# Compression matmuls in four column groups of the array, and another order of work where two blocks meet

## The chip, the cores and the metric

One Trainium2 chip, one of its cores. The metric is the device time of one execution in microseconds (us). Between runs of this kernel the time varies by about 0.05%.

## What is computed

Two layers, each a mixer and an MLP, over 256 positions of width 2048, in float32. The mixer projects the normalised input into the heads of four kinds of attention, runs them, and projects back. The part that the change touches first is the compression of the first kind:

```python
blk = np.arange(n_c)[:, None] * NSA_CMP_STRIDE + np.arange(NSA_CMP_BLOCK)[None, :]

def compress(t, pe, w1, w2):
    tb = (t[:, blk] + pe).reshape(b, n_c, NSA_CMP_BLOCK * d)
    return jax.nn.gelu(tb @ w1) @ w2

kc = compress(k_cmp, pe_k, cmp_k1, cmp_k2)
vc = compress(v_cmp, pe_v, cmp_v1, cmp_v2)
```

There are 15 blocks of 32 positions with stride 16, d is 128, and w1 has 32 x 128 rows and 256 columns. So `tb @ w1` is a sum over 32 positions of a 15 x 128 by 128 x 256 product, done for keys and for values in both layers. The second part of the change lies where a block ends in `x = x + _rms_norm(...)` and the next begins with `hin = _rms_norm(x, g)` and a product with its first weights.

## The kernel before

All weights come from memory in granules of at most 128 x 1024 float32 (`Granule`), in the order in which they are used. `load` issues their DMAs on SP into six `raw` buffers. `prep` splits a granule into two tiles, `hi` and `lo`, in a format that TensorE multiplies in one pass: `split_hi` (L190) copies raw to hi on ACT, and `split_lo` (L193) subtracts on DVE. There are six hi and six lo buffers, and `ready(g, look)` sees to it that everything up to `look` granules ahead of g is split. The normalised input is kept in the same way in the tiles `HL`, high half and low half of each chunk. A product with weights is then hi x (high and low input together, 512 columns, L424) and lo x high input (256 columns, L429).

The program is written out in full when it is built, in a fixed order on each engine. A list `work` gives the granules' order. `run_gran` takes one granule: it first lets waiting work of the vector engines go on (`fill("v")`), then readies and multiplies, then lets waiting small matmuls go on (`fill("pe")`). Small work (evacuations, attention, norms) is written as generators (`Chain`) that these calls advance.

**Compression.** `cmp_units` gives 8 granules for each of keys and values in each layer, 32 in all, and `mixer` puts one of them after every second granule of the projections. `build_t2` adds pe to the 15 blocks' inputs and writes for each position 32 columns into a tile `T2`, 15 high parts and 15 low parts. A compression granule holds four positions. For each, two matmuls take 128 columns of T2 from the position's first on as stationary operand and hi or lo (256 columns) as moving one, and all accumulate in one bank (L1060):

```python
for w in (g.hi, g.lo):
    TE.matmul(box["a"][:, :256], lhsT=lt, rhs=w[:, j * 256:(j + 1) * 256],
```

Rows 0 to 31 of the bank are used: `cmp_tail` copies them to `hs` (L1075), adds the high parts' rows and the low parts' by a float32 matmul with the constant `sel` (L1080, 32 rows), applies gelu and multiplies by w2.

**Joins.** `start_block` begins a block. The first is `run_first`; the three others are `lead`, whose pieces run between the last matmuls of the block before. x is held in two tiles (t = 0 and 1) of four chunks of 512 columns. `res` adds the block's result to a chunk of x on DVE, `t_in` transposes it on TensorE (L376), `hl_in` makes HL of it on ACT and DVE (L384, L385), and `sq_in` squares it on ACT for the norm (L391). The block's first three units are multiplied as their parts become ready: `mm_t` and `mm_lo` (L461, L465) with chunks 0 and 1, `mm_w` (L416, L417, L419) with chunks 2 and 3. After the last of them `finish` launches `rows`: DVE sums the squares (L485, L313), POOL takes the power and makes a diagonal tile (L314, L488), TensorE spreads it over all partitions with a float32 matmul (L493), and ACT copies the result to `r2bc` (L495). The units' evacuations (L906 on ACT and L908 on DVE in a mixer) follow.

Of the kernel before, what the change touches and what calls it, by code (L numbers as in the profile page):

```python
# [56 lines left out]
def _const_tables():  # L57
# [16 lines left out]
    for b in range(15):  # L74
        sel[b, b] = 1.0
        sel[16 + b, b] = 1.0
    put("sel", sel)
# [30 lines left out]
class Granule:  # L108
    __slots__ = ("src", "n", "uses", "raw", "hi", "lo", "idx")

    def __init__(self, src, n):
        self.src, self.n, self.uses = src, n, 1

# [23 lines left out]
def hybrid_kernel(ctx, tc, a):  # L137
# [26 lines left out]

    def gran(src, c0, n):
        return Granule(src[:, c0:c0 + n], n)

# [11 lines left out]
    def load(upto):  # L179
        while state["load"] <= min(upto, len(grans) - 1):  # L180
            g = grans[state["load"]]
            g.raw = wp.tile([128, 1024], F32, tag="raw", name="raw", bufs=RAW_BUFS)
            nc.sync.dma_start(out=g.raw[:, :g.n], in_=g.src)
            state["load"] += 1
# [14 lines left out]
    def prep(upto, how=split):  # L199
        while state["gran"] <= min(upto, len(grans) - 1):  # L200
            i = state["gran"]
            if i >= HL_BUFS and grans[i - HL_BUFS].uses > 0:
                return
            g = grans[i]
            load(i + RAW_BUFS - 1)
            g.hi, g.lo = split_tiles()
            how(g, 0, g.n)
            state["gran"] += 1
# [266 lines left out]
    def start_block(site, src, evacs, mg, mg_extra=None):  # L475
# [25 lines left out]
        def finish(accs, first):  # L501
            scaled[0] = False
            launch(rows())
            for i in range(len(us)):
                launch(evacs[i](accs[i], first and first[i]))
# [36 lines left out]
        def lead():  # L542
# [41 lines left out]
            split_lo(gs[2, 0], 0, 1024)  # L584
            prep(gs[0, 1].idx, split_hi)
            t_in(2, 0)
            t_in(2, 1)
            hl_in(site, 2)
            split_lo(gs[0, 1], 0, 1024)
            for i in range(n):  # L590
# [4 lines left out]
            prep(gs[1, 1].idx)  # L595
            res(mg, 3, 1)
            accs = [bank() for _ in us]
            for c in (2, 3):
                for i in range(n):
                    g = gs[i, 1]  # L600
                    ready(g, 4)
                    mm_w(accs[i], g, 4 * c, 4 * c + 4, 8, EARLY)
                    used(g)
                    if c == 2 and i == 0:
                        t_in(3, 0)
                        t_in(3, 1)
                        hl_in(site, 3)
                    for q in {(2, 1): ((0, 1), (1, 1)), (2, 2): ((2, None), (3, 0)), (3, 0): ((3, 1),)}.get((c, i), ()):
                        sq_in(q[0], (0, 1) if q[1] is None else q[1:])
            finish(accs, first)  # L610
# [246 lines left out]
    def mixer(l):  # L857
# [5 lines left out]
        def open_pool():  # L863
# [6 lines left out]
            st["oT"] = [mp.tile([128, 256], F32, name=f"oT{k}") for k in range(KT)]  # L870
            st["T2"] = [mp.tile([128, 608], F32R, name=f"T2{i}") for i in range(2)]
            for t_ in st["T2"]:
                GP.memset(t_.bitcast(F32), 0.0)
            st["Pc"] = [scr([128, 4, 128], f"Pc{i}") for i in range(2)]
# [151 lines left out]
        def build_t2(kind, half):  # L1026
            yield "v", dict(scr=1)
            src = st["kc" if kind == 0 else "vc"]
            tmp = scr([128, 16, 16], "t2tmp")
            v_ = src[:, 16 * half:16 * half + 240].rearrange("p (b s) -> p s b", s=16)  # L1030
            pe = st["pe"][:, kind, 16 * half:16 * half + 16].unsqueeze(2).to_broadcast([128, 16, 15])
            V.tensor_tensor(tmp[:, :, :15], v_, pe, op=OP.add)
            T = st["T2"][half]
            t3 = T[:, :512].rearrange("p (s c) -> p s c", c=32)
            V.tensor_copy(t3[:, :, 0:15], tmp[:, :, :15])
            V.tensor_tensor(t3[:, :, 16:31], tmp[:, :, :15], t3[:, :, 0:15].bitcast(F32), op=OP.subtract)
            st["T2", kind, half] = True
            drop("scr")
            if half:
                drop("qk")  # L1040

        def cmp_units(kind):
            box = {}

            def make(u4):
                u = a["cmp1"][l, kind, u4]
                for h in range(2):
                    g = gran(u, h * 1024, 1024)

                    def run(g=g, p0=8 * u4 + 4 * h):  # L1050
                        def emit():
# [4 lines left out]
                            for j in range(4):  # L1056
                                pos = p0 + j
                                lt = st["T2"][pos // 16][:, (pos % 16) * 32:(pos % 16) * 32 + 128]
                                for w in (g.hi, g.lo):
                                    TE.matmul(box["a"][:, :256], lhsT=lt, rhs=w[:, j * 256:(j + 1) * 256],  # L1060
                                              start=(pos == 0 and w is g.hi), stop=(pos == 31 and w is g.lo))
                        run_gran(g, 0.85, emit)
# [9 lines left out]
        def cmp_tail(kind, p):  # L1072
            yield "v", dict(scr=1)
            hs = scr([128, 512], "hs")
            SC.activation(hs[:32, :256], p[:32, :256], AF.Copy)  # L1075
            drop("ps")
            yield "pe", dict(ps=1)
            q = bank()
            for j in range(2):
                TE.matmul(q[:, j * 128:(j + 1) * 128], lhsT=hs[:32, j * 128:(j + 1) * 128],  # L1080
                          rhs=C("sel")[:32], start=True, stop=True)
            yield "v"
# [532 lines left out]
```

## Time and profile before

| | |
|---|---|
| time, median of 3 runs | 2319.83 us (2318.98 to 2320.26) |
| the profiled execution's own time | 2319.57 us |
| span of its profile | 2317.4 us |
| PE, weight loads, DVE, ACT, POOL busy | 99%, 86%, 74%, 52%, 2% of the span |
| granted TensorE clock, mean | 0.999 |
| bytes moved | 437.57 MB, 189 GB/s |

The span runs from the first to the last instruction in the trace; the time has what lies around it as well. PE is TensorE's multiplying, PEld its loading of weights, which overlaps with it. The end of a matmul is modelled in the trace and overlaps with the next one's start, so what a matmul takes of TensorE's stream is read from the distance between starts, or from the chain of waits, which gives each piece of time to one instruction.

### The profile page before, as it was taken

The numbers are of one execution on the slowest core, as the hardware profiler recorded it, in microseconds if no ns is written. First come the engines' busy times: TensorE is split into PE (matmuls) and PEld (weight loads), VectorE is DVE, ScalarE is ACT, GpSimd is POOL, SyncE is SP. The second block draws the span as 40 slices with busy tenths as digits, with TensorE's granted clock in tenths as the row PEclk, the third lists the DMA queues.
The fourth block names the chain that finished last, engine by engine and source line by source line (L and its number), as shares of the span: only waits on it lengthen the run. The fifth ranks groups of instructions, "written<-read, shape, count | busy, mean of one in ns | idle before, by whom it ended". The sixth has DMA issues, their size and how long they took to land.

```text
span 2317.4 us, 33362 instructions
## 1 busy us (share of the span) xinstructions
PE 2298.9 (99%) x12476; PEld 1994.7 (86%) x12476; DVE 1720.3 (74%) x2936; ACT 1202.1 (52%) x1947; POOL 51.0 (2%) x71
## 2 busy tenths in 40 slices
PE   8999999999999999999999999999999999999998
PEld 8888888888888888888888888888888888888887
DVE  6967656798888888565588676568988888885655
ACT  6654555644444444555466545555444444444553
POOL 1000000100000000000010000001000000000000
PEclk9999999999999999999999999999999999999999
DMA  8764456556555555656557644564666555555563
GB/s 275 253 217 136 147 170 202 167 190 201 191 191 185 189 190 184 200 187 210 173 180 237 208 146 155 173 194 155 201 200 192 190 190 191 184 193 197 193 200 116
DMA packets 122659, 437.57 MB, mean 189 GB/s; under 512 B 13888, under 2 KB 14016, under 8 KB 122496
## 3 DMA queue, kind: packets, MB, share of 16 engines
q1 hardware_dynamic: 120384, 429.40, 56.3%
q0 software_dynamic: 1824, 5.94, 0.8%
q8 instruction: 98, 1.61, 0.3%
q14 instruction: 65, 0.53, 0.1%
q10 hardware_dynamic: 288, 0.10, 0.0%
HBM read 433.28 MB, written 2.10 MB: 188 GB/s over the span
## 4 chain that ended last, share of the span: by engine, by line
PE 96%; DVE 2%; ACT 1%; issue 1%; POOL 0%; DMA 0%; SPq 0%; DVEq 0%; POOLq 0%; ACTq 0%
PE bank L424 36%; PE bank L429 19%; PE bank L715 9%; PE bank L713 9%; PE bank L714 9%; PE bank L665 2%; PE bank L667 2%; PE bank L666 2%; PE bank L1060 1%; PE bank L1137 1%; DVE lo L193 1%; PE bank L417 1%; DVE x L405 0%; PE bank L461 0%; ACT trash L391 0%
## 5 line engine op out<-in xcount | busy, mean ns | idle before, releaser
L193 DVE TENSOR_TENSOR lo<-raw,hi 128x1024 fp32r<-128x1024 f32 (+1 forms) x818 | 984.6, 1210 | 489.2 <-ACT hi L190 484.1
L190 ACT ACTIVATE hi<-raw 128x1024 fp32r<-128x1024 f32 (+1 forms) x818 | 847.2, 1046 | 410.8 <-PE bank L715 265.4
L424 PE MATMUL bank<-HL,hi 128*128 128x512 f32 x3648 | 881.8, 392 | 0.0
L424 PEld LDWEIGHTS bank<-HL,hi 128*128 128x128 f32 x3648 | 668.5, 188 | 128.5
L429 PEld LDWEIGHTS bank<-HL,lo 128*128 128x128 f32 x3648 | 470.0, 191 | 18.1
L429 PE MATMUL bank<-HL,lo 128*128 128x256 f32 x3648 | 480.7, 283 | 0.0
L713 PE MATMUL bank<-hi,xs 128*128 128x512 f32 x960 | 374.4, 390 | 0.0
L715 PE MATMUL bank<-hi,xs 128*128 128x512 f32 x960 | 373.6, 389 | 0.0
L714 PE MATMUL bank<-lo,xs 128*128 128x512 f32 x960 | 373.5, 389 | 0.0
L715 PEld LDWEIGHTS bank<-hi,xs 128*128 128x128 f32 x960 | 180.2, 188 | 37.6
L714 PEld LDWEIGHTS bank<-lo,xs 128*128 128x128 f32 x960 | 180.2, 188 | 37.2
L713 PEld LDWEIGHTS bank<-hi,xs 128*128 128x128 f32 x960 | 180.2, 188 | 37.0
L1486 DVE SCALAR_TENSOR_TENSOR cv<-u,cw,cv 128x255 f32<-128x255 f32 x352 | 170.2, 483 | 12.5
L1472 ACT ACTIVATE u<-bank 128x256 f32<-128x256 f32 x176 | 66.6, 381 | 207.6 <-PE bank L424 196.1
L1492 ACT ACTIVATE gl<-cv 128x256 f32<-128x256 f32 x88 | 36.8, 418 | 217.8 <-DVE cv L1486 217.7
L665 PE MATMUL bank<-hi,HL 128*128 128x512 f32 (+1 forms) x256 | 97.3, 380 | 1.5 <-DVE qk L908 1.5
L667 PE MATMUL bank<-hi,HL 128*128 128x512 f32 (+1 forms) x256 | 93.6, 366 | 0.0
L666 PE MATMUL bank<-lo,HL 128*128 128x512 f32 (+1 forms) x256 | 93.3, 365 | 0.0
L1480 DVE TENSOR_TENSOR u<-u,r2bc 128x256 f32<-128x256 f32 x176 | 74.9, 426 | 5.7
L1483 DVE TENSOR_SCALAR cv<-u,cw 128x256 f32<-128x256 f32 x176 | 72.7, 413 | 6.4
L1474 DVE TENSOR_TENSOR u<-u,bank 128x256 f32<-128x256 f32 x176 | 72.9, 414 | 0.0
L686 DVE TENSOR_TENSOR xs<-y,xs 128x256 fp32r<-128x256 f32 x176 | 72.2, 418 | 0.0
(216 smaller groups left out, 1486.7 us busy)
## 6 DMA issues: line engine op xcount, KB each, us to landing
raw<-in_w_up SPq DMA_DIRECT2D x352, 512.0 KB, 4.3
raw<-in_w_down SPq DMA_DIRECT2D x176, 512.0 KB, 3.7
raw<-in_w_cols SPq DMA_DIRECT2D x122, 512.0 KB, 4.3
raw<-in_w_out SPq DMA_DIRECT2D x64, 512.0 KB, 4.1
raw<-in_w_v SPq DMA_DIRECT2D x48, 512.0 KB, 4.0
raw<-in_cmp SPq DMA_DIRECT2D x32, 512.0 KB, 5.0
gpost<-in_gpost POOLq DMA_DIRECT2D x8, 512.0 KB, 6.4
raw<-in_w_x SPq DMA_DIRECT2D x8, 408.0 KB, 4.6
```

The lines of the kernel that those rows point to most:

```text
L190: SC.activation(g.hi[:, c0:c0 + n], g.raw[:, c0:c0 + n], AF.Copy)
L193: eng.tensor_tensor(g.lo[:, c0:c0 + n], g.raw[:, c0:c0 + n], g.hi[:, c0:c0 + n].bitcast(F32), op=OP.subtract)
L424: TE.matmul(o, lhsT=g.hi[:, k % 8 * 128:k % 8 * 128 + 128], rhs=HL[k // 4][:, k % 4, :], start=(k == 0), stop=(k == KT - 1))
L429: TE.matmul(o[:, :256], lhsT=g.lo[:, k % 8 * 128:k % 8 * 128 + 128], rhs=hview(k), start=False, stop=False)
L665: TE.matmul(o, lhsT=h, rhs=wh, start=(K == 0), stop=False)
L666: TE.matmul(o, lhsT=h, rhs=wl, start=False, stop=False)
L667: TE.matmul(o, lhsT=lo, rhs=wh, start=False, stop=(K == KT - 1))
L713: TE.matmul(o, lhsT=h_, rhs=wh, start=(k[1] == 0), stop=False)
L714: TE.matmul(o, lhsT=h_, rhs=wl, start=False, stop=False)
L715: TE.matmul(o, lhsT=l_, rhs=wh, start=False, stop=(k[1] == nk - 1))
L1480: V.tensor_tensor(u, u, r2bc, op=OP.mult)
L1486: V.scalar_tensor_tensor(cv[:, n:], u[:, :256 - n], w[:, tap:tap + 1], cv[:, n:], op0=OP.mult, op1=OP.add)
```

## The change

A compression granule is no longer split. It is marked `whole`, its four positions are multiplied straight from `raw` in float32, each with a 32-column piece of T2 into 32 partitions of the bank of its own, so each of the four uses 32 columns of the array. T2 holds float32 values, 16 columns a position. `cmp_tail` copies all 128 rows and `sel` adds four partial sums. A load into the raw buffer of a whole granule is written only after that granule's matmuls. In `lead`, squares and one `split_lo` stand earlier, `ready` looks two granules ahead instead of four at one place, and `rows` is launched and advanced once after the second-last `mm_w` instead of in `finish`.

```diff
     for b in range(15):
-        sel[b, b] = 1.0
-        sel[16 + b, b] = 1.0
+        sel[b::32, b] = 1.0
...
     def load(upto):
         while state["load"] <= min(upto, len(grans) - 1):
-            g = grans[state["load"]]
+            i = state["load"]
+            if i >= RAW_BUFS and grans[i - RAW_BUFS].whole and grans[i - RAW_BUFS].uses > 0:
+                return
+            g = grans[i]
...
             load(i + RAW_BUFS - 1)
-            g.hi, g.lo = split_tiles()
-            how(g, 0, g.n)
+            if state["load"] <= i:
+                return
+            if not g.whole:
+                g.hi, g.lo = split_tiles()
+                how(g, 0, g.n)
...
         def finish(accs, first):
-            scaled[0] = False
-            launch(rows())
+            if first is None:
+                scaled[0] = False
+                launch(rows())
...
             prep(gs[0, 1].idx, split_hi)
+            sq_in(0, (1,))
+            split_lo(gs[0, 1], 0, 1024)
             t_in(2, 0)
             t_in(2, 1)
             hl_in(site, 2)
-            split_lo(gs[0, 1], 0, 1024)
...
             res(mg, 3, 1)
+            sq_in(1, (1,))
             accs = [bank() for _ in us]
+            after = {(2, 0): ((2, 0),), (2, 1): ((3, 0), (2, 1)), (2, 2): ((3, 1),)}
             for c in (2, 3):
                 for i in range(n):
                     g = gs[i, 1]
-                    ready(g, 4)
+                    ready(g, 4 if i or c == 3 else 2)
                     mm_w(accs[i], g, 4 * c, 4 * c + 4, 8, EARLY)
                     used(g)
...
-                    for q in {(2, 1): ((0, 1), (1, 1)), (2, 2): ((2, None), (3, 0)), (3, 0): ((3, 1),)}.get((c, i), ()):
-                        sq_in(q[0], (0, 1) if q[1] is None else q[1:])
+                    for q, t in after.get((c, i), ()):
+                        sq_in(q, (t,))
+                    if c == 3 and i == 1:
+                        scaled[0] = False
+                        launch(rows())
+                        fill("v")
             finish(accs, first)
...
-            st["T2"] = [mp.tile([128, 608], F32R, name=f"T2{i}") for i in range(2)]
+            st["T2"] = [mp.tile([128, 320], F32, name=f"T2{i}") for i in range(2)]
...
-            V.tensor_tensor(tmp[:, :, :15], v_, pe, op=OP.add)
-            T = st["T2"][half]
-            t3 = T[:, :512].rearrange("p (s c) -> p s c", c=32)
-            V.tensor_copy(t3[:, :, 0:15], tmp[:, :, :15])
-            V.tensor_tensor(t3[:, :, 16:31], tmp[:, :, :15], t3[:, :, 0:15].bitcast(F32), op=OP.subtract)
+            T = st["T2"][half][:, :256].rearrange("p (s c) -> p s c", c=16)
+            V.tensor_tensor(T[:, :, 0:15], v_, pe, op=OP.add)
...
-                                pos = p0 + j
-                                lt = st["T2"][pos // 16][:, (pos % 16) * 32:(pos % 16) * 32 + 128]
-                                for w in (g.hi, g.lo):
-                                    TE.matmul(box["a"][:, :256], lhsT=lt, rhs=w[:, j * 256:(j + 1) * 256],
-                                              start=(pos == 0 and w is g.hi), stop=(pos == 31 and w is g.lo))
+                                c = (p0 + j) % 16 * 16
+                                TE.matmul(box["a"][32 * j:32 * j + 32, :256], lhsT=st["T2"][p0 // 16][:, c:c + 32],
+                                          rhs=g.raw[:, j * 256:(j + 1) * 256], start=(p0 == 0), stop=(p0 == 28))
...
-            SC.activation(hs[:32, :256], p[:32, :256], AF.Copy)
+            SC.activation(hs[:, :256], p[:, :256], AF.Copy)
...
-                TE.matmul(q[:, j * 128:(j + 1) * 128], lhsT=hs[:32, j * 128:(j + 1) * 128],
-                          rhs=C("sel")[:32], start=True, stop=True)
+                TE.matmul(q[:, j * 128:(j + 1) * 128], lhsT=hs[:, j * 128:(j + 1) * 128],
+                          rhs=C("sel"), start=True, stop=True)
```

The lines of the changed kernel are shifted: its L1066 is the compression matmul, L429 and L434 are L424 and L429 of before, L195 is L193, L390 is L385, L410 is L405, L490 is L485.

On TensorE, at the first compression granule, before:

```order
L424 MATMUL bank<-HL_123,hi 128x512 x4
L1060 MATMUL bank<-hi,T_105 128x256
L1060 MATMUL bank<-lo,T_105 128x256
L1060 MATMUL bank<-hi,T_105 128x256
L1060 MATMUL bank<-lo,T_105 128x256
L1060 MATMUL bank<-hi,T_105 128x256
L1060 MATMUL bank<-lo,T_105 128x256
L1060 MATMUL bank<-hi,T_105 128x256
L1060 MATMUL bank<-lo,T_105 128x256
L424 MATMUL bank<-HL_120,hi 128x512 x4
```

and now:

```order
L434 MATMUL bank<-HL_122,lo 128x256 x4
L434 MATMUL bank<-HL_123,lo 128x256 x4
L429 MATMUL bank<-HL_122,hi 128x512 x4
L429 MATMUL bank<-HL_123,hi 128x512 x4
L1066 MATMUL bank<-raw,T_105 32x256 x4
L429 MATMUL bank<-HL_120,hi 128x512 x4
```

Eight matmuls that write all 128 rows have become four that write 32 rows each, in the same place between two runs of 512-column matmuls.

On DVE, at the join from mixer 0 to MLP 0, before (HL_4163 and HL_4164 are chunks 2 and 3 of the input):

```order
L440 SCALAR_TENSOR_TENSOR HL_4162<-bank,gpre,HL_4162 128x128 x4
L193 TENSOR_TENSOR lo<-raw,hi 128x1024
L385 SCALAR_TENSOR_TENSOR HL_4163<-bank,gpre,HL_4163 128x256 x4
L193 TENSOR_TENSOR lo<-raw,hi 128x1024 x2
L405 SCALAR_TENSOR_TENSOR x_69<-mg_4112,rr_78,x_69 128x512
L193 TENSOR_TENSOR lo<-raw,hi 128x1024 x3
L385 SCALAR_TENSOR_TENSOR HL_4164<-bank,gpre,HL_4164 128x256 x4
L193 TENSOR_TENSOR lo<-raw,hi 128x1024 x2
L485 TENSOR_REDUCE r_82<-ss_76 128x2
```

and now (chunks 2 and 3 are HL_4023 and HL_4024):

```order
L445 SCALAR_TENSOR_TENSOR HL_4022<-bank,gpre,HL_4022 128x128 x4
L195 TENSOR_TENSOR lo<-raw,hi 128x1024 x2
L390 SCALAR_TENSOR_TENSOR HL_4023<-bank,gpre,HL_4023 128x256 x4
L195 TENSOR_TENSOR lo<-raw,hi 128x1024
L410 SCALAR_TENSOR_TENSOR x_69<-mg_3972,rr_78,x_69 128x512
L195 TENSOR_TENSOR lo<-raw,hi 128x1024
L390 SCALAR_TENSOR_TENSOR HL_4024<-bank,gpre,HL_4024 128x256 x4
L195 TENSOR_TENSOR lo<-raw,hi 128x1024 x3
L490 TENSOR_REDUCE r_82<-ss_76 128x2
```

One lo has moved ahead of chunk 2, and two have moved from before chunk 3 to behind it.

On ACT, at the join from MLP 0 to mixer 1, before (L391 are the squares, L906 the copy out of an accumulator):

```order
L190 ACTIVATE hi<-raw 128x1024
L384 ACTIVATE HL_11140<-bank,gpre 128x256 x4
L190 ACTIVATE hi<-raw 128x1024 x4
L384 ACTIVATE HL_11141<-bank,gpre 128x256 x4
L190 ACTIVATE hi<-raw 128x816
L391 ACTIVATE trash,ss_76<-x_69 128x512 x2
L391 ACTIVATE trash,ss_76<-x_68 128x512
L391 ACTIVATE trash,ss_76<-x_69 128x512
L391 ACTIVATE trash,ss_76<-x_68 128x512
L391 ACTIVATE trash,ss_76<-x_69 128x512
L190 ACTIVATE hi<-raw 128x816
L1388 ACT_TABLE_LOAD
```

and now (the squares are L396, hi is L192, the HL pieces L389):

```order
L192 ACTIVATE hi<-raw 128x1024
L396 ACTIVATE trash,ss_76<-x_69 128x512
L389 ACTIVATE HL_11000<-bank,gpre 128x256 x4
L192 ACTIVATE hi<-raw 128x1024
L396 ACTIVATE trash,ss_76<-x_69 128x512
L192 ACTIVATE hi<-raw 128x1024
L389 ACTIVATE HL_11001<-bank,gpre 128x256 x4
L396 ACTIVATE trash,ss_76<-x_68 128x512
L192 ACTIVATE hi<-raw 128x1024 x2
L192 ACTIVATE hi<-raw 128x816
L396 ACTIVATE trash,ss_76<-x_68 128x512
L396 ACTIVATE trash,ss_76<-x_69 128x512 x2
```

Of the six squares that stood together, three now stand ahead of them, between other pieces of work.

## Rows read from the trace of the kernel before

**Rows 1.** The page, part 1: busy time, share of the span, instructions.
```profile
PE 2298.9 (99%) x12476; PEld 1994.7 (86%) x12476; DVE 1720.3 (74%) x2936; ACT 1202.1 (52%) x1947; POOL 51.0 (2%) x71
```

**Rows 2.** The page, part 4: the chain that ended last, by engine.
```profile
PE 96%; DVE 2%; ACT 1%; issue 1%; POOL 0%; DMA 0%; SPq 0%; DVEq 0%; POOLq 0%; ACTq 0%
```

**Rows 3.** The chain in order of time, compression of layer 0: start us, us, what.
```profile
51.97 1.84 PE bank L424 x8
53.80 0.97 PE bank L1060 x8
54.77 1.84 PE bank L424 x8
...
60.37 0.97 PE bank L1060 x8
```

**Rows 4.** PE's groups of instructions: count, busy us, mean ns, idle before.
```profile
L1060 PE MATMUL bank<-hi,T 128*128 128x256 f32 x128 | 32.3, 285 | 0.0
L1060 PE MATMUL bank<-lo,T 128*128 128x256 f32 x128 | 31.8, 282 | 0.0
```

**Rows 5.** The chain in order of time: three places with float32 matmuls.
```profile
108.61 0.45 PE bank L1137 x4
...
111.85 0.86 PE bank L1137 x4
...
195.91 0.22 PE bank L1244 x2
```

**Rows 6.** The timeline there: start us, us, engine, line, form, [idle before].
```profile
101.74 0.52 PEld L1080 LDWEIGHTS bank<-cst,hs 32*128 32x128 f32 x4 [0.35 <-issue]
...
111.69 1.02 PE L1137 MATMUL bank<-qk 128*128 128x256 f32 x4
...
195.77 0.36 PE L1244 MATMUL bank<-nlf,cst 128*128 128x4 f32 x2
```

**Rows 7.** The chain in order of time, around one L1080.
```profile
99.97 1.84 PE bank L424 x8
101.81 0.64 PE bank L1080 x4
102.45 1.58 PE bank L424 x6
```

**Rows 8.** The page, part 5: the splits (busy us, mean ns of one, idle before).
```profile
L193 DVE TENSOR_TENSOR lo<-raw,hi 128x1024 fp32r<-128x1024 f32 (+1 forms) x818 | 984.6, 1210 | 489.2 <-ACT hi L190 484.1
L190 ACT ACTIVATE hi<-raw 128x1024 fp32r<-128x1024 f32 (+1 forms) x818 | 847.2, 1046 | 410.8 <-PE bank L715 265.4
```

**Rows 9.** DMA issues of compression weights, and busy us of each engine, 53 to 113 us.
```profile
raw<-in_cmp SPq DMA_DIRECT2D x32, 512.0 KB, 5.0
...
53.00:113.00 60.00, 60.00 (x374) 53.90 (x373) 54.72 (x116) 36.40 (x60) 0.00 (x0) 1.00 0.75 255
```

**Rows 10.** The timeline at the first join, chunk 2.
```profile
432.96 2.35 DVE L193 TENSOR_TENSOR lo<-raw,hi 128x1024 fp32r<-128x1024 f32 x2
...
433.41 0.39 PE L417 MATMUL bank<-HL,hi 128*128 128x512 f32 x1
...
434.23 0.39 PE L419 MATMUL bank<-HL,lo 128*128 128x256 f32 x1 [0.43 <-DVE lo L193]
```

**Rows 11.** The timeline at the first join, chunk 3.
```profile
435.89 3.49 DVE L193 TENSOR_TENSOR lo<-raw,hi 128x1024 fp32r<-128x1024 f32 x3
...
439.32 0.28 PE L416 MATMUL bank<-HL,lo 128*128 128x256 f32 x1
439.83 0.50 PE L417 MATMUL bank<-HL,hi 128*128 128x512 f32 x1 [0.23 <-DVE HL L385]
...
440.56 0.28 PE L416 MATMUL bank<-HL,lo 128*128 128x256 f32 x1
440.86 0.50 PE L417 MATMUL bank<-HL,hi 128*128 128x512 f32 x1
```

**Rows 12.** The timeline of POOL at the first join.
```profile
448.58 0.72 POOL L314 TENSOR_TENSOR r<-r,cst 128x2 f32<-128x2 f32 x1 [19.83 <-DVE r L313]
449.40 2.69 POOL L488 TENSOR_SCALAR diag<-cst,r 128x128 f32<-128x128 f32 x2
```

**Rows 13.** The timeline at the second join: ACT, DVE and PE.
```profile
1177.36 0.62 ACT L391 ACTIVATE trash<-x 128x512 bf16<-128x512 f32 x1
...
1181.67 0.19 ACT L391 ACTIVATION_READ_ACCUMULATOR trash<-x 128x1 f32 x1
...
1185.68 1.93 DVE L193 TENSOR_TENSOR lo<-raw,hi 128x816 fp32r<-128x816 f32 x2 [1.73 <-ACT hi L190]
...
1186.26 0.29 PE L667 MATMUL bank<-hi,HL 128*128 128x272 f32 x1
...
1187.53 0.41 DVE L908 TENSOR_TENSOR qk<-qk,bank 128x256 f32<-128x256 f32 x1
...
1188.09 0.36 PE L665 MATMUL bank<-hi,HL 128*128 128x272 f32 x1 [1.54 <-DVE qk L908]
```

More of the change, by code (lines that the diff above doesn't have):

```diff
@@ L108, with __init__ @@
 class Granule:
-    __slots__ = ("src", "n", "uses", "raw", "hi", "lo", "idx")
-    def __init__(self, src, n):
-        self.src, self.n, self.uses = src, n, 1
+    __slots__ = ("src", "n", "uses", "raw", "hi", "lo", "idx", "whole")
+    def __init__(self, src, n, whole=False):
+        self.src, self.n, self.uses, self.whole = src, n, 1, whole
 class Chain:
@@ L163, in hybrid_kernel, with gran @@
     state = dict(load=0, gran=0)
-    def gran(src, c0, n):
-        return Granule(src[:, c0:c0 + n], n)
+    def gran(src, c0, n, whole=False):
+        return Granule(src[:, c0:c0 + n], n, whole)
     def add(f, *gs):
@@ L870, in open_pool @@
             st["oT"] = [mp.tile([128, 256], F32, name=f"oT{k}") for k in range(KT)]
-            st["T2"] = [mp.tile([128, 608], F32R, name=f"T2{i}") for i in range(2)]
+            st["T2"] = [mp.tile([128, 320], F32, name=f"T2{i}") for i in range(2)]
             for t_ in st["T2"]:
-                GP.memset(t_.bitcast(F32), 0.0)
+                GP.memset(t_, 0.0)
             st["Pc"] = [scr([128, 4, 128], f"Pc{i}") for i in range(2)]
@@ L1026, in build_t2 @@
         def build_t2(kind, half):
-            yield "v", dict(scr=1)
+            yield "v"
             src = st["kc" if kind == 0 else "vc"]
-            tmp = scr([128, 16, 16], "t2tmp")
             v_ = src[:, 16 * half:16 * half + 240].rearrange("p (b s) -> p s b", s=16)
             pe = st["pe"][:, kind, 16 * half:16 * half + 16].unsqueeze(2).to_broadcast([128, 16, 15])
-            V.tensor_tensor(tmp[:, :, :15], v_, pe, op=OP.add)
-            T = st["T2"][half]
-            t3 = T[:, :512].rearrange("p (s c) -> p s c", c=32)
-            V.tensor_copy(t3[:, :, 0:15], tmp[:, :, :15])
-            V.tensor_tensor(t3[:, :, 16:31], tmp[:, :, :15], t3[:, :, 0:15].bitcast(F32), op=OP.subtract)
+            T = st["T2"][half][:, :256].rearrange("p (s c) -> p s c", c=16)
+            V.tensor_tensor(T[:, :, 0:15], v_, pe, op=OP.add)
             st["T2", kind, half] = True
-            drop("scr")
             if half:
@@ L1047, in make @@
                 for h in range(2):
-                    g = gran(u, h * 1024, 1024)
+                    g = gran(u, h * 1024, 1024, True)
                     def run(g=g, p0=8 * u4 + 4 * h):
```

## The prediction

> **What bounds the kernel now.** I read the busy times first: TensorE is busy for 2298.9 of 2317.4 us [rows 1]. The chain of work that ended last says the same: 96% of it is PE, and no other engine has more than 2% [rows 2]. So what the change takes from TensorE's own stream is gained in full, what it takes from ACT or DVE is gained only where TensorE waits for them, and the places to read are two: the compression's matmuls and the joins between blocks. The profiled execution took 2319.57 us around its span of 2317.4; the median of the runs shown is 2319.83. I sum against the first and add the 0.26 us at the end. A measurement of this kernel can tell about 0.2% from no change, that is 4.6 us.
>
> In the compression, a granule (four positions) is eight matmuls and takes 0.97 us of TensorE, with unbroken work on both sides [rows 3]. There are 256 such matmuls, so 32 granules [rows 4]: 31 us in all.
>
> **The change, part A: four column groups.** A granule becomes four float32 matmuls of 256 columns into 32 array columns each. What a float32 matmul costs here is seen at L1137: two of them with 256 columns are four passes and take 0.86 us, so a pass takes 0.215 us and each matmul two passes [rows 5, 6]. Four matmuls are eight passes: 1.72 us one after another, and 0.43 us if the four groups run beside each other. Everything hangs on which, and no row of this trace shows column groups, so I bound it from both sides.
>
> What the trace does show is a change of the array's shape. The L1080 matmuls use 32 of 128 rows. Four of their passes take 0.64 us, where four ordinary passes of 128 columns take 0.45 [rows 5, 7]; and the six matmuls behind them take 1.58 us where six of eight that took 1.84 would be 1.38 [rows 7]. That is 0.19 us on the way in and 0.20 on the way out, 0.39 for the pair. On the way in the weights stand in the open (the weight loader was idle for 0.35 us before them [rows 6]). A load of 128 columns costs 0.11, as L1244 shows, whose two passes move 4 columns each and still take 0.22 [rows 5, 6]. With 32 columns I estimate a quarter, 0.03, so 0.19 becomes 0.11 and the pair 0.31. The change now pays this pair at each of the 32 granules, where before there was none. The Trainium skill, "TensorEngine Tiling (Array Packing)", section "Tiling Modes", says that a change of tiling mode drains TensorE; the 0.39 us at L1080 agrees, and without that rule the sum would be 32 times 0.31, 9.9 us, lower.
>
> With the groups beside each other the last group starts six load-and-pass steps after the first: 6 x 0.03 = 0.17 us (0.11 each would be 0.66, the far bound). A granule is then 0.31 + 0.17 + 0.43 = 0.91 us, against 0.97: 32 x -0.06 = **-1.9 us**. Its bounds are 0.43 us (no drain, no steps: -17.3 us) and 2.03 us (all eight passes in a row: +33.9 us). I take the lower half because the four groups write different partitions of one bank and share no weights.
>
> The end of each compression (four in all) now multiplies 128 instead of 32 rows of hs. The passes have the same columns, but the pair of shape changes goes: 4 x -0.39 = **-1.6 us**. The copy into hs has as many elements per partition as before.
>
> The hi and lo passes of 32 granules go: 1.05 us of ACT and 1.2 of DVE each [rows 8]. I count them at nothing, because TensorE has no gap in the compression [rows 3]. In return a whole granule keeps its raw buffer until TensorE has read it, and every later load queues behind it on SP. Six places later comes the next compression granule but one, some 13 us on (53.80 to 60.37 is one period) [rows 3]; a load lands 5.0 us after issue [rows 9], and the two ordinary ones behind it, by 3 x 512 KB at the 255 GB/s of that stretch [rows 9], some 4 us later, then hi and lo. That leaves about 2 us, so nothing is added; if the reserve were 1 us short instead, TensorE would lose up to 1 us at each of the 32 granules. build_t2 loses two DVE operations, and the T2 memsets on POOL shrink; nothing waits for either.
>
> **Part B: the joins.** There are three (after mixer 0, MLP 0 and mixer 1), all alike but for one wait. At the first, L419 starts 0.82 us after the L417 before it instead of 0.23: it waits for the lo of the first second-half granule, which DVE computes after the four L385 of chunk 2 [rows 10]. The change puts that lo first, into a stretch where DVE waits for ACT; the loss of 0.59 goes. Then the first L417 of chunk 3 starts 0.51 us after its L416 instead of 0.12, and one later 0.30 after [rows 11], because three lo (3.49 us) stand on DVE before the L385 of chunk 3 [rows 11]. The smaller look-ahead leaves one lo there; the L385 are done 2.4 us earlier, before TensorE asks: 0.39 + 0.18. So 1.16 us at a join. The moved squares (0.8 us each on ACT) use ACT's idle time before the chunk's transposes; what is late next is L493, which now stands eight L424 and eight L429 earlier, 2.8 us of TensorE, and needs POOL's power and diag first, 0.72 and 2.69 us [rows 12]. Their start follows the last square, which comes some 4 us earlier as well, so by my count they end 1 us before TensorE gets there.
>
> At the second join a longer wait follows: after three matmuls of x0 TensorE stands from 1186.26 to 1188.09, until L908 has emptied an accumulator bank [rows 13]. L908 is behind two lo that wait for hi, and ACT is late with hi because six squares (1177.36 to 1181.86, 0.75 each) stand in a row [rows 13]. Three of them move ahead: -2.25 us on ACT. One more lo (1.0 us) now stands before L908, so L908 ends some 1.25 earlier, at 1186.7. The three matmuls (0.37) have then to be done, but L493 (0.43) already is: TensorE gains 0.9 + 0.43 = 1.35 us there, and the 1.16 from earlier in this join are inside it. Together 2 x 1.16 + 1.35 = **-3.7 us**. Bounds: 0, or a new wait of 1 us at each L493 (+3), and all waits gone, -6.
>
> **Sum.** 2319.57 - 1.9 - 1.6 - 3.7 = 2312.4; for the median 2312.6, 0.3% faster. Without the granules' own part the change gains 5.3 us, so it breaks even at a granule of 0.97 + 5.3/32 = 1.14 us, is faster by over 0.2% below 0.99 and slower by over 0.2% above 1.28.
>
> **The rivals.**
> 1. *Passes overlap in pairs only* (slower). In the trace matmuls start in program order on one stream [rows 3, 5]. The two passes of one group need the same columns, and the first pass of the next group stands behind the second of this one. Then each slot of 0.215 us holds one group's second pass and the next one's first: five slots and the shape change, 1.38 us, 32 x +0.41 = +13.3 us, 2327.8. It decides from 1.14 us on. For it: the program order; against: the four groups share nothing. The Trainium skill, "TensorE: Matmul & The Clock Gate", Part 3, says that matmuls start and end strictly in order, which speaks for this rival; its table gives 2.38 times for three column tiles, one matmul in each, which only says that groups do overlap.
> 2. *No overlap* (slower): 0.31 + 1.72 = 2.03 us, +33.9, 2348.4. For it only that no row shows an overlap.
> 3. *The joins give nothing*, because L493 or the reordered DVE queue makes a wait of the same size: 2312.6 + 3.7 = 2316.3, no change.
> 4. *Column groups need no drain* or hide it: 0.43 to 0.6 us, 2297 to 2303. Against it: L1080.
>
> **How the numbers follow.** Forecast 0.46, rivals 0.25, 0.10, 0.09 and 0.10. The forecast's own range is 2308 to 2317, so about 0.07 of it lies within 0.2%. Faster: 0.39 + 0.10 = 0.49; the same: 0.07 + 0.09 = 0.16; slower: 0.25 + 0.10 = 0.35. The range 2302 to 2331 leaves out rival 2 and half of rival 4.
>
> **What would show it.** The chain's row for the new matmul: below 0.99 us per granule is right, 1.4 is rival 1, 2.0 rival 2. L1080's successor without the 0.20 behind it; L419 0.23 us after L417; no idle time of PE before the first L417 of chunk 3; L665 of x0 free by 1187 on the old clock. A wait of PE for a raw load in the compression, or for diag at L493, would make the forecast wrong.

## The result and the profile after

The change makes the kernel faster: 2307.69 us, median of 4 runs (2307.63 to 2308.07), against 2319.78 us for the kernel before on the same chip, a ratio of 0.9949 with a 95% interval of 0.9937 to 0.9961. The gain is 12.1 us where 7.2 were forecast. The time lies inside the stated range of 2302 to 2331, and just below the forecast's own 2308 to 2317. The span went from 2317.4 to 2305.9 us. In the changed kernel L1066 is the compression matmul, L1086 the one with sel, L498 the one that spreads the norm's factor; L192 and L195 are the splits.

The page, parts 1 and 4 (as [rows 1, 2]) and the splits of part 5 (as [rows 8]):

```profile
PE 2290.0 (99%) x12476; PEld 1969.2 (85%) x12476; DVE 1680.8 (73%) x2888; ACT 1171.9 (51%) x1915; POOL 49.0 (2%) x71
...
PE 96%; ACT 1%; DVE 1%; issue 1%; POOL 0%; DMA 0%; SPq 0%; DVEq 0%; POOLq 0%; ACTq 0%
...
L195 DVE TENSOR_TENSOR lo<-raw,hi 128x1024 fp32r<-128x1024 f32 (+1 forms) x786 | 947.8, 1210 | 513.6 <-ACT hi L192 508.4
L192 ACT ACTIVATE hi<-raw 128x1024 fp32r<-128x1024 f32 (+1 forms) x786 | 815.5, 1046 | 413.4 <-PE bank L728 265.4
```

The bound is the same: 96% of the chain is PE, 12476 matmul records as before. The 32 splits fewer (786 for 818) are seen on ACT and DVE.

The chain in order of time in the compression of layer 0, and around one matmul with sel (start us, us, what), which answers to [rows 3, 7]:

```profile
52.40 1.84 PE bank L429 x8
54.24 0.57 PE bank L1066 x8
54.81 2.04 PE bank L429 x8
...
60.61 0.57 PE bank L1066 x8
...
100.74 0.44 PE bank L1086 x4
101.18 1.83 PE bank L429 x8
```

A granule takes 0.57 us, and the eight matmuls behind it 2.04 instead of 1.84: 0.77 us instead of 0.97. By the starts of the same matmuls in both traces the 32 granules gain 0.16 to 0.20 us each, by what stands behind them, and 0.18 on average. The period from granule to granule falls here from 6.57 to 6.37 us. L1086 has neither the 0.64 nor the 0.20 behind it any more.

The timeline of one granule (start us, us, engine, line, form), and L1066 as a source line (ns, shortest, median and longest):

```profile
90.79 0.16 PEld L1066 LDWEIGHTS bank<-raw,T 128*32 128x32 f32 x8
...
90.79 0.64 PE L1066 MATMUL bank<-raw,T 128*32 128x256 f32 x8
```

```profile
L1066 PEld LDWEIGHTS bank<-raw,T x256: 106/108/109, 54.2 to 1293.8; 128*32 128x32 f32 x128
L1066 PE MATMUL bank<-raw,T x256: 379/391/404, 54.2 to 1294.0; 128*32 128x256 f32 x128
```

Each load takes 0.11 us, yet eight of them lie within 0.16: they run beside each other. In the single records behind this row the first four passes, one of each group, start at 90.793, 90.800, 90.806 and 90.813 us, 7 ns apart, and the four others at 91.033 to 91.053, 240 ns later.

To split the gain, I compared the start of the same matmul in both traces at some places. The start of the kernel is 0.42 us later, a shift that other traces show too (0.1 to 1.2 us, before any part that was changed). From there the compression of mixer 0 gains 3.66 us and that of mixer 1 3.68; the three joins gain 1.04, 2.51 and 1.08. That sums to the 11.5 us of the spans. So the compression gave 7.3 us (forecast 3.5) and the joins 4.6 (forecast 3.7).

The timeline at the first join, chunks 2 and 3, and the next block's start, which answers to [rows 10 to 12]:

```profile
425.59 2.35 DVE L195 TENSOR_TENSOR lo<-raw,hi 128x1024 fp32r<-128x1024 f32 x2
...
430.15 0.40 PE L422 MATMUL bank<-HL,hi 128*128 128x512 f32 x1
430.38 0.28 PE L424 MATMUL bank<-HL,lo 128*128 128x256 f32 x1
...
434.36 0.88 DVE L390 SCALAR_TENSOR_TENSOR HL<-bank,gpre,HL 128x256 fp32r<-128x256 f32 x2 [0.15 <-ACT HL L389]
...
435.48 0.28 PE L421 MATMUL bank<-HL,lo 128*128 128x256 f32 x1
435.60 0.39 PE L422 MATMUL bank<-HL,hi 128*128 128x512 f32 x1
...
441.58 1.99 POOL L493 TENSOR_SCALAR diag<-cst,r 128x128 f32<-128x128 f32 x2
443.04 2.51 DVE L195 TENSOR_TENSOR lo<-raw,hi 128x1024 fp32r<-128x1024 f32 x2 [0.53 <-ACT hi L192]
445.22 0.60 PE L498 MATMUL bank<-diag,cst 128*128 128x256 f32 x2
445.47 0.41 DVE L1480 TENSOR_TENSOR u<-u,bank 128x256 f32<-128x256 f32 x1
446.02 2.06 PE L429 MATMUL bank<-HL,hi 128*128 128x512 f32 x8 [0.21 <-DVE u L1480]
```

L424 (L419 before) follows its L422 by 0.23 us, and no L422 of chunk 3 waits: the first follows its L421 by 0.12 us, where it was 0.51. The diag is there at 443.57, 1.65 us before L498 asks for it. But the L429 behind L498 now waits for a bank that DVE empties with L1480, after two lo: this join gains 1.48 us up to L498 and gives 0.43 back.

The timeline at the second join (answers to [rows 13]):

```profile
1175.93 1.01 DVE L195 TENSOR_TENSOR lo<-raw,hi 128x816 fp32r<-128x816 f32 x1 [0.41 <-ACT hi L192]
...
1178.95 1.93 DVE L195 TENSOR_TENSOR lo<-raw,hi 128x816 fp32r<-128x816 f32 x2 [2.01 <-ACT hi L192]
...
1180.23 0.60 PE L498 MATMUL bank<-diag,cst 128*128 128x256 f32 x2
...
1180.80 0.41 DVE L921 TENSOR_TENSOR qk<-qk,bank 128x256 f32<-128x256 f32 x1
1180.86 0.38 ACT L500 ACTIVATE r2bc<-bank 128x256 f32<-128x256 f32 x1 [0.62 <-PE bank L498]
...
1181.36 0.36 PE L678 MATMUL bank<-hi,HL 128*128 128x272 f32 x1 [0.53 <-ACT r2bc L500]
```

This join began 4.28 us earlier than in the trace before. Put back on the old clock, L921 (L908 before) runs at 1185.08, not 1187.53. The lo that I had added to its wait ran at 1175.93, in time that DVE spends waiting for ACT: it still waits 2.01 us for the next hi. TensorE no longer waits for L921 here. The wait of 1.54 us is gone, and a shorter one, 0.53 us, is left, which the trace puts down to L500, the copy out of L498's bank.

### The profile page after: what moved, and what is told of

Same layout as the page of the kernel before. It is cut to its first block, busy times and chain, and to the rows that moved or that the text cites. A ratio compares the mean times of both kernels' runs of the same rounds, so it can differ in the third digit from the quotient of the medians.

```text
span 2305.9 us, 33201 instructions
## 1 busy us (share of the span) xinstructions
PE 2290.0 (99%) x12476; PEld 1969.2 (85%) x12476; DVE 1680.8 (73%) x2888; ACT 1171.9 (51%) x1915; POOL 49.0 (2%) x71
## 4 chain that ended last, share of the span: by engine, by line
PE 96%; ACT 1%; DVE 1%; issue 1%; POOL 0%; DMA 0%; SPq 0%; DVEq 0%; POOLq 0%; ACTq 0%
PE bank L429 36%; PE bank L434 19%; PE bank L726 9%; PE bank L727 9%; PE bank L728 9%; PE bank L678 2%; PE bank L680 2%; PE bank L679 2%; PE bank L1143 1%; PE bank L1066 1%; PE bank L422 1%; ACT hi L192 1%; PE bank L466 0%; PE bank L381 0%; DVE x L410 0%
## 5 line engine op out<-in xcount | busy, mean ns | idle before, releaser
L195 DVE TENSOR_TENSOR lo<-raw,hi 128x1024 fp32r<-128x1024 f32 (+1 forms) x786 | 947.8, 1210 | 513.6 <-ACT hi L192 508.4
L192 ACT ACTIVATE hi<-raw 128x1024 fp32r<-128x1024 f32 (+1 forms) x786 | 815.5, 1046 | 413.4 <-PE bank L728 265.4
L429 PE MATMUL bank<-HL,hi 128*128 128x512 f32 x3648 | 883.1, 392 | 0.4 <-DVE u L1480 0.4
L429 PEld LDWEIGHTS bank<-HL,hi 128*128 128x128 f32 x3648 | 668.4, 188 | 132.5 <-ACT qk L919 3.3
L434 PEld LDWEIGHTS bank<-HL,lo 128*128 128x128 f32 x3648 | 469.5, 191 | 23.8 <-DVE qk L921 4.1
L434 PE MATMUL bank<-HL,lo 128*128 128x256 f32 x3648 | 481.4, 283 | 0.0
L1480 DVE TENSOR_TENSOR u<-u,bank 128x256 f32<-128x256 f32 x176 | 73.0, 414 | 0.0
```

What stands on the lines that cost most here:

```text
L192: SC.activation(g.hi[:, c0:c0 + n], g.raw[:, c0:c0 + n], AF.Copy)
L195: eng.tensor_tensor(g.lo[:, c0:c0 + n], g.raw[:, c0:c0 + n], g.hi[:, c0:c0 + n].bitcast(F32), op=OP.subtract)
L429: TE.matmul(o, lhsT=g.hi[:, k % 8 * 128:k % 8 * 128 + 128], rhs=HL[k // 4][:, k % 4, :], start=(k == 0), stop=(k == KT - 1))
L434: TE.matmul(o[:, :256], lhsT=g.lo[:, k % 8 * 128:k % 8 * 128 + 128], rhs=hview(k), start=False, stop=False)
```

## The experiments

**The two parts apart.** First the column groups alone (`finish` and `lead` as in the kernel before; parts of that edit are shown), then the order at the joins alone (the compression as before):

```diff
-            sq_in(0, (1,))
-            split_lo(gs[0, 1], 0, 1024)
             t_in(2, 0)
...
-                    ready(g, 4 if i or c == 3 else 2)
+                    ready(g, 4)
...
-                    if c == 3 and i == 1:
-                        scaled[0] = False
-                        launch(rows())
-                        fill("v")
```

> The changed kernel with lead and finish as before, so the column groups alone. From the two traces I put 7.3 us of the 12.1 on the compression and 4.6 on the joins. Theory (the two parts add up): 2312.4 us, that is 7.3 under the kernel before. Rival (the joins gain only because DVE and ACT no longer split compression granules, or the parts share a gain): near 2307.7, the changed kernel's own time.

> The kernel before with the new lead and finish alone. Theory: 4.6 us under the kernel before, 2315.2, of it 1.0, 2.5 and 1.1 at the three joins. Rival: less than 2 us, if the gain at the second join needs the compression's relief on DVE.

The groups alone took 2311.93 us, ratio 0.9968 (0.9956 to 0.9979), the joins alone 2314.86 us, ratio 0.9981 (0.9971 to 0.999), with the kernel before at 2319.44. That is 7.5 and 4.6 us, together the whole gain. Measured on the same matmuls, the compressions give 3.7 and 3.6 us in the first (and its joins nothing), the joins 1.02, 2.50 and 1.10 in the second. Neither part needs the other.

**What makes a granule cheap: one group.** All four positions go to group 0, and hs and sel have 32 rows again:

```diff
+  q = 0
-  TE.matmul(box["a"][32 * j:32 * j + 32, :256], ..., start=(p0 == 0), stop=(p0 == 28))
+  TE.matmul(box["a"][32 * q:32 * q + 32, :256], ..., start=(p0 == 0 and j == 0), stop=(p0 == 28 and j == 3))
```

> All four positions of a granule go to the first column group and the same 32 rows of the bank; the end of a compression copies and multiplies 32 rows as before. Theory (each column group is a stream of its own, and the gain is that four run beside each other): eight passes in a row, 0.31 + 8 x 0.215 = 2.0 us a granule instead of 0.77, 32 x 1.25 + 4 x 0.4 = 41.6 us more than the changed kernel, 2349. Rival (narrow float32 matmuls are cheap by themselves, whatever the group): 0.8 us a granule, 2309.

It took 2350.25 us in one run. The chain in order of time (L1067 is the compression matmul here and in the next two runs):

```profile
52.64 1.84 PE bank L429 x8
54.48 1.84 PE bank L1067 x8
56.32 2.04 PE bank L429 x8
```

1.84 + 0.20 = 2.04 us a granule, and its passes start 0.22 us apart. The same matmuls cost 1.27 us less when they have four column groups.

**Two groups, in two orders.** Positions 0 and 2 in one group, 1 and 3 in the other; then 0 and 1 in one, 2 and 3 in the other. In both, hs and sel have 64 rows, and `start` and `stop` are set for each group:

```diff
+  q = j % 2
-  TE.matmul(box["a"][32 * j:32 * j + 32, :256], ...
+  TE.matmul(box["a"][32 * q:32 * q + 32, :256], ...
```

```diff
+  q = j // 2
-  TE.matmul(box["a"][32 * j:32 * j + 32, :256], ...
+  TE.matmul(box["a"][32 * q:32 * q + 32, :256], ...
```

> As the change, but with two column groups instead of four: positions 0 and 2 go to group 0, 1 and 3 to group 1, and 64 rows of hs and sel are added up. Theory (each group runs its own passes one after another at 0.215 us, the groups beside each other, in whatever order the program has them): four passes in a group, so 0.43 us more a granule than with four groups, about 1.2 us in the chain with what stands behind it; 32 x 0.43 = 13.8 us more than the change, and up to 1.6 us more for the 64-row shape of the sel matmuls: 2321.5 to 2323.1 us. Rival (passes start strictly in program order, so that only the second pass of one matmul and the first of the next overlap): five slots of 0.215 and the shape change, 1.38 us, some 2327 us; but that rival gave 1.38 for four groups as well, where 0.77 was measured.

> As the run before it (two column groups), but positions 0 and 1 go to group 0, 2 and 3 to group 1, so in program order the four passes of group 0 stand ahead of those of group 1. Theory (a pass that has to wait for its group does not hold up what stands behind it, as deep as four matmuls): the same as with alternating groups, about 1.2 us a granule, 2321.5 to 2323.1 us. Rival (a waiting pass holds up what is behind it; the overlap comes only where neighbours in program order belong to different groups): group 1 starts when the last pass of group 0 has been let go, seven slots of 0.215 us and the shape change, about 1.8 us a granule, 32 x 1.0 = 32 us over the change, some 2340 us.

They took 2322.46 and 2322.61 us (one run each). The chain of the second; the first shows the same 0.99 and 2.07:

```profile
53.66 0.99 PE bank L1067 x8
54.66 2.07 PE bank L429 x8
```

So 1.22 us in either order. In the second the two matmuls of group 0 stand ahead of those of group 1 in the program; yet the eight passes start in pairs, 14 ns apart, and a pair every 0.215 us. Four slots leave no room for group 1 to start after group 0's second matmul, which needs seven: a matmul of a free column group starts before an earlier one that waits for its own. The records do not name a pass's group; the order follows from the number of slots.

**What the shape change costs: granules side by side.** Two granules after every fourth projection granule, then four after every eighth:

```diff
-        at = [CMP_AT + round(i * CMP_STEP) for i in range(len(c))]
+        at = [CMP_AT + 2 * CMP_STEP * (i // 2) for i in range(len(c))]
```

```diff
+        at = [CMP_AT + 4 * CMP_STEP * (i // 4) for i in range(len(c))]
```

> The changed kernel with compression granules put into the order of work two at a time, after every fourth granule instead of one after every second. Theory (each run of column-group matmuls pays one change of the array's shape, some 0.3 us, whatever its length): 16 changes fewer, -4.8 us, 2302.9; a pair takes 0.31 + 4 x 0.24 = 1.27 us. Rival (the price is per matmul, not per change of shape): 2307.7. A third way: raw buffers, held until TensorE reads them, make loads late and TensorE waits for them: over 2307.7.

> As the change, but four compression granules stand next to each other after every eighth granule instead of one after every second. Theory (one change of shape in and out for each stretch of 32-column work, 0.31 to 0.35 us, and 0.43 us for each granule in it): eight changes fewer than with pairs, so 2.5 to 2.9 us under the 2302.0 of the pairs, about 2299.3 us; the chain's row for the compression matmul about 1.9 us for x32. Rival (the raw buffers decide): four of the six raw buffers are held until TensorE has read them, the next loads are issued late, and TensorE waits behind each of the eight stretches for hi or lo, by 1 us or more each: 2307 us or above, with idle time of PE behind the compression put down to a split or a DMA.

The pairs took 2302.01 us, ratio 0.9925 (0.991 to 0.994): 5.7 us less than the change, for 16 shape changes fewer. Measured on the same matmuls the two compressions gain 5.45 us, 0.34 for each change of shape. The chain, 1.00 + 0.23 = 1.23 us for a pair:

```profile
54.48 1.00 PE bank L1066 x16
55.48 2.07 PE bank L429 x8
```

The quads took 2324.55 us, ratio 1.0022 (1.0012 to 1.0031): the rival was right that holding four raw buffers costs more than it brings, though not at each stretch. The chain, the timeline of ACT and PE, and the busy times by stretch (us, PE, PEld, DVE, ACT, POOL, clock, DMA share, GB/s):

```profile
53.72 1.86 PE bank L1066 x32
55.58 2.04 PE bank L429 x8
```

```profile
81.56 1.06 ACT L192 ACTIVATE hi<-raw 128x1024 fp32r<-128x1024 f32 x1 [0.81 <-DMA raw<-in_w_cols]
82.92 1.06 ACT L192 ACTIVATE hi<-raw 128x1024 fp32r<-128x1024 f32 x1 [0.30 <-DMA raw<-in_w_cols]
83.88 0.36 ACT L1081 ACTIVATE hs<-bank 128x256 f32<-128x256 f32 x1
...
84.30 1.22 PE L1086 MATMUL bank<-cst,hs 128*128 128x128 f32 x4 [2.87 <-ACT hs L1081]
```

```profile
78.00:81.50 3.50, 3.43 (x27) 2.37 (x16) 2.65 (x8) 2.75 (x9) 0.00 (x0) 1.00 0.85 286
81.50:84.30 2.80, 0.00 (x0) 0.00 (x1) 2.66 (x10) 2.38 (x3) 0.00 (x0) 0.85 0.91 262
84.30:87.00 2.70, 2.70 (x8) 2.34 (x9) 2.49 (x4) 1.38 (x2) 0.00 (x0) 0.50 1.02 417
87.00:90.00 3.00, 3.00 (x11) 2.58 (x10) 0.91 (x1) 2.96 (x5) 0.00 (x0) 0.50 1.02 411
90.00:95.00 5.00, 5.00 (x37) 4.66 (x36) 3.36 (x6) 2.60 (x5) 0.00 (x0) 0.97 0.66 238
```

The matmuls do what the theory says: 1.86 + 0.20 = 2.06 us for four granules, so 0.34 once and 0.43 for each. The time is lost at the four ends of a compression. There ACT has hi before it whose raw tiles were loaded late, and the copy into hs stands behind them. TensorE stands for 2.87, 3.90, 4.13 and 4.78 us, 15.7 in all. Within the first wait its granted clock falls to 0.50, the lower of its two levels (1.2 GHz), and stays there until about 90.3 us. At the four places TensorE works for 6.0, 3.4, 5.9 and 2.9 us at that level. Half of that, 9.1 us, is my estimate of what the clock costs; with the waits it makes 24.8 of the 25.3 us by which the run misses 2299.3.

**The quads with hs first.** To the quads two things are added: the look-ahead is cut around the last four granules of a compression, and loads are issued again right after each granule:

```diff
-    def run_gran(g, us, emit):
+    def run_gran(g, us, emit, look=LOOK):
         fill("v")
-        ready(g)
+        ready(g, state.pop("look", look))
         emit()
         used(g)
+        load(state["gran"] + RAW_BUFS - 1)
...
-                        run_gran(g, 0.85, emit)
+                        run_gran(g, 0.85, emit, {20: 4, 24: 3, 28: 2}.get(p0, LOOK))
                         if p0 == 28:
+                            state["look"] = 2
```

> The quads kernel with one thing put right: around the last four granules of a compression the look-ahead of the splits is cut (to the granules whose raw tiles have been loaded by then), so that the copy into hs and the gelu stand on ACT ahead of the hi that wait for late loads, not behind them. Theory (the quads lost their time only there: TensorE stood 2.87, 3.90, 4.13 and 4.78 us before its sel matmuls, 15.7 us in all, and the clock it got back was 0.50 for some 6 us after that): the four waits go and with them the slow stretches, so about 2299.3 us, the 2.5 to 2.9 us under the pairs that eight changes of shape fewer are worth; no PE idle before L1088 or L1100 and a granted clock of 1.00 throughout. Rival (holding four of six raw buffers starves TensorE itself): with hs out of the way TensorE waits for hi or lo of the granules behind the compression instead, some us at each of the four places, 2306 us or more.

It took 2300.87 us, ratio 0.9918 (0.9902 to 0.9935), 23.7 less than the quads. The four waits and the slow stretches are gone. The copy into hs now stands at 79.74 us, ahead of the hi that come late, while their raw tiles landed no earlier than in the quads (the first two at 82.38 and 83.62 us, against 81.48 and 82.84). So it was the order on ACT that made TensorE wait. 1.6 us are missing to the forecast. 1.2 of them are two waits of the same kind further on: the matmuls with the compressed keys (L1118) wait for a copy on ACT that stands behind four hi. The other 0.4 I did not trace. The timeline, then the clock in that stretch:

```profile
79.74 0.36 ACT L1083 ACTIVATE hs<-bank 128x256 f32<-128x256 f32 x1
...
88.61 2.05 PE L1118 MATMUL bank<-cmp,qk 128*128 128x128 f32 x16 [0.69 <-ACT cmp L1105]
...
1230.37 2.05 PE L1118 MATMUL bank<-cmp,qk 128*128 128x128 f32 x16 [0.54 <-ACT cmp L1105]
```

```profile
88.00:89.00 1.00, 0.39 (x3) 0.39 (x4) 1.00 (x2) 0.97 (x3) 0.00 (x0) 1.00 1.01 401
89.00:95.00 6.00, 6.00 (x43) 5.55 (x43) 5.49 (x17) 2.27 (x8) 0.00 (x0) 1.00 0.88 290
```

**The sel matmuls by themselves.** The kernel before, with all 128 rows of hs and sel:

```diff
-            SC.activation(hs[:32, :256], p[:32, :256], AF.Copy)
+            SC.activation(hs[:, :256], p[:, :256], AF.Copy)
...
-                TE.matmul(q[:, j * 128:(j + 1) * 128], lhsT=hs[:32, j * 128:(j + 1) * 128],
-                          rhs=C("sel")[:32], start=True, stop=True)
+                TE.matmul(q[:, j * 128:(j + 1) * 128], lhsT=hs[:, j * 128:(j + 1) * 128],
+                          rhs=C("sel"), start=True, stop=True)
```

> The kernel before with one edit: hs is copied with all 128 rows and the four small float32 matmuls with sel use all 128 rows (the further rows of sel are zero), so that they have the full shape of the array. Theory (the pair of shape changes around them cost 0.39 us at each of the four compressions, and nothing else hangs on it): 1.6 us less, about 2317.9 us; in the chain 0.44 instead of 0.64 us for x4 and no 0.20 behind them. Rival (the 0.40 us that the change gained there came from another order of its compression granules): 2319.5 us as before.

2318.51 us, ratio 0.9994 (0.9985 to 1.0004): by itself no difference that the time can tell. The trace can: measured on the same matmuls each mixer's compression gains 0.78 and 0.80 us, 1.6 in all. The chain:

```profile
103.04 0.44 PE bank L1080 x4
103.48 1.83 PE bank L424 x8
```

**The splits kept.** The change, with hi and lo of the compression granules still written and not read:

```diff
-            if not g.whole:
-                g.hi, g.lo = split_tiles()
-                how(g, 0, g.n)
+            g.hi, g.lo = split_tiles()
+            how(g, 0, g.n)
```

> The change, but every compression granule is still split on ACT and DVE into hi and lo that nobody reads (32 x 1.05 us of ACT and 32 x 1.2 us of DVE more). Theory (TensorE has no gap in the compression, so the splits that the change saves were worth nothing): 2307.7 us, the same as the change. Rival (the relief of ACT and DVE is a part of the gain): slower than the change, by up to the 3 us that the compressions gained more than was forecast, 2310.5 us.

2308.53 us, ratio 0.9951 (0.9936 to 0.9966), the change's within the error. In the trace the splits cost 1.2 us in mixer 0, at one place, where the matmuls with the compressed keys wait for a copy on ACT, and nothing in mixer 1. The timeline:

```profile
106.63 2.05 PE L1115 MATMUL bank<-cmp,qk 128*128 128x128 f32 x16 [0.99 <-ACT cmp L1102]
```

**rows one unit later.** The change, with `launch(rows())` in `finish` again:

```diff
         def finish(accs, first):
-            if first is None:
-                scaled[0] = False
-                launch(rows())
+            scaled[0] = False
+            launch(rows())
...
-                    if c == 3 and i == 1:
-                        scaled[0] = False
-                        launch(rows())
-                        fill("v")
```

> The change with one part undone: rows (the norm's factor, with its matmul L493 of the kernel before) is launched by finish again, one unit later, at all three joins. Theory (at the first and the third join the earlier float32 matmul takes an accumulator bank, so that the next 512-column matmul meets a bank that DVE has not yet emptied, and gives back 0.43 us): measured on the same matmuls, 0.4 us less than the change at the first join and at the third; at the second join, where the matmul then stands behind the wait again, 0.4 us more; together 2307.3 us, no difference that the time can tell. Rival (the bank is late for another reason, the two lo ahead of the evacuation on DVE): the wait stays, no difference at joins one and three.

2306.5 us in one run, too little a difference for the time to tell. On the same matmuls the first join is 0.47 us shorter than in the change and the third 0.49; the second is 0.08 longer, not the 0.4 expected. The timeline at the first join: no wait behind L498.

```profile
446.69 1.11 PE L434 MATMUL bank<-HL,lo 128*128 128x256 f32 x8
447.64 0.59 PE L498 MATMUL bank<-diag,cst 128*128 128x256 f32 x2
447.88 1.30 PE L434 MATMUL bank<-HL,lo 128*128 128x256 f32 x8
```

**All of it together.** Quads, hs first with the look-ahead cut for one granule more, and rows late:

```diff
-        ready(g, state.pop("look", look))
+        ready(g, state["look"].pop() if state["look"] else look)
...
-                            state["look"] = 2
+                            state["look"] = [2, 2]
```

> The run with quads and hs first, with two more edits: the look-ahead stays cut for one granule more, so that the copy of the compressed keys and values stands on ACT ahead of the four hi that wait for late loads, and rows is launched one unit later at the joins. Theory (the parts add up): the waits of 0.69 and 0.54 us in the compression go, and the joins give what the run with late rows gave over the change, 0.9 us: 2300.9 - 1.2 - 0.9 = 2298.8 us, the shortest of all kernels here. Rival (the look-ahead cut that far makes lo or hi late for TensorE behind the compression): 2300 us or more, with idle time of PE put down to a split within 15 us behind a compression.

2298.16 us (2297.54 to 2298.81), ratio 0.9907 (0.9891 to 0.9924): the fastest kernel here, 9.5 us under the change. TensorE has no wait left in either compression or behind L498 at the first and third joins. On the same matmuls the compressions are 2.78 us shorter than with pairs, for eight changes of shape fewer: 0.35 each, the 2.5 to 2.9 us that the quads were to bring.

## Why the prediction was right, and where its sizes were off

**The bound** was right: what left TensorE's stream was gained in full, and what left ACT and DVE was worth next to nothing (2308.53 us with the splits kept, and a wait at one place that costs 1.2 us).

**The granule** had the right sign and mechanism and the wrong size: 0.77 us instead of 0.91, -5.7 us (7.3 less 1.6) instead of -1.9. Of its three terms the passes were right: 0.43 us for each granule of a stretch. The shape change is what the quads leave once, 0.34, and 0.34 by the pairs too, where 0.31 was estimated. The term that failed is the "six load-and-pass steps" at 0.03 us, 0.17 in all: I took the loads as following one another, scaled by columns. They run beside each other, and the last group starts 0.02 us after the first. Had the step been left out, the granule would have been 0.74. The two errors have opposite signs, so a small part of the step's was hidden.

**The sel matmuls**, -1.6 us, were exact, by a row of the kernel before alone [rows 7].

**The raw buffers** were rightly counted at nothing: no wait for a load in the compression. The reserve that I worked out, some 2 us, was not measured by itself; the quads show what happens without one.

**The joins** gave -4.6 for -3.7. At the first and third the waits that I listed went and a little more (1.48 for 1.16), but I looked for the new wait at the wrong instruction. L498 found its diag ready; it is the matmul behind it that meets a full bank, and that gives back 0.43. Launching rows one unit later removes that wait, so the earlier launch is a part of the change that costs 0.9 us. At the second join the term of 1.35 was mis-sized (and its sum, 0.9 + 0.43, is 1.33): it measured 2.51. "One more lo (1.0 us) now stands before L908" was wrong, because that lo fits into DVE's wait for ACT, and so L921 runs 2.45 us earlier where 1.25 was forecast. Nor are "the 1.16 from earlier in this join" inside the term: with the long wait gone they count in full, 1.4 us up to there, and the rest is the 1.54 us that became 0.53. The 0.43 that I credited to L493 being done is not there, since the late rows lose only 0.08.

**The rivals.** The first, pairs of passes only, gave 1.38 us a granule and 0.77 was measured. It rested on program order, and the two orders of two groups show that order between groups does not decide. The Trainium skill, "TensorE: Matmul & The Clock Gate", Part 3, says that matmuls start and end strictly in order; for float32 matmuls in different column groups these traces do not agree (four slots of 0.215 us where that order needs seven). The second, no overlap, is what one column group gives: 2.04 us for the 2.03 forecast. The third, nothing at the joins, is excluded by the joins alone (0.9981, interval below 1). The fourth, no drain, is excluded by the pairs: a change of shape costs TensorE 0.34 us. The Trainium skill, "TensorEngine Tiling (Array Packing)", section "Tiling Modes", says that a change of tiling mode drains TensorE; a cost for each change, whatever the length of the stretch, agrees with that.

## What to carry to other kernels

Four column groups ran their float32 passes beside each other here (0.43 us for eight passes, 1.73 in one group), and what remains of the cost is the change of shape (0.34 us): put the matmuls of one shape next to each other, as far as the buffers that they hold allow. Where an in-order engine holds both look-ahead work and a small copy that TensorE waits for, cut the look-ahead there; holding four of six buffers turned a forecast gain of some 3 us over the pairs into a loss of 22 by such a queue, and with the look-ahead cut far enough the compressions gave 2.8. When a matmul is moved forward, ask not only for its inputs but also for the bank that the one behind it will need.

## What the hardware showed that was not expected

- Loads of 32 columns for four column groups start 7 ns apart although each lasts 0.11 us, and so do their passes. With one group the passes start 0.216 us apart, and its first two loads 28 ns apart: there too a load starts before the one ahead of it has ended.
- A matmul of a free column group starts before an earlier one in the program whose group is busy: 2322.46 and 2322.61 us for the two orders, four slots of 0.215 us in both.
- In or just after each of TensorE's four waits in the quads, 2.87 to 4.78 us long, its granted clock fell to 0.50. A longer wait did not mean a longer stretch at that level: after 2.87 us the engine worked for 6.0 us at 0.50, after 4.78 us for 2.9. Waits of 0.99 us (with the splits kept) and 1.54 us (at the second join before) left it at 1.00. What lies between was not tried.
